# Hymba decoder step on one core: the order of the second norm and of the operand work inside a norm slot

## The chip, the cores and the metric

The kernel runs on one core of one Trainium2 chip. The metric is device time in microseconds (us) for one launch of the whole program, the span of the core's instructions and what lies around it. Below, PE is the matrix engine (TensorE), PEld its weight loads, DVE is VectorE, ACT is ScalarE, POOL is GpSimd, and SP is SyncE, which issues the DMAs.

## The reference

One decoder layer is computed for a prompt of 2048 tokens and for 8 x 4 sample tokens that share its weights (model width 1024). Attention and a spatial gate come first; their outputs are joined, multiplied by `w_out` and added to `x`. The part that the change touches follows:

```python
x = x + jnp.concatenate([att, u * gate], axis=-1) @ w_out
x = x + _swiglu(x, norm2_g, w_gate, w_up, w_down)

def _rmsnorm(x, g):
    y = x * lax.rsqrt(jnp.mean(x * x, axis=-1, keepdims=True) + EPS)
    return y * g

def _swiglu(x, g, w_gate, w_up, w_down):
    h = _rmsnorm(x, g)
    return (jax.nn.silu(h @ w_gate) * (h @ w_up)) @ w_down
```

A final norm of `x` gives the output. All of it is float32.

## The kernel before

Every float32 matrix is split into a high part and a rest (`xh` and `xl`, `wh` and `wl`), and a product is made of three matmuls: high by high, high by low, low by high. The gate and up products use a scheme with seven products of combined operands in the place of eight (`TOK` in `product` says which operand each takes). So each normed tile of 128 tokens must be turned (transposed), combined and split into seven high and seven low operands before the products can start.

The 16 tiles of 128 tokens are worked through in three blocks of 6, 6 and 4 tiles; the 32 sample rows are a fifth, small tile of the last block. For each block the program does this:

1. `open_unit` multiplies half 0 of `w_out` for each tile. The sums wait in PSUM banks (PSUM is the memory that PE writes its sums to).
2. `second_phase` goes over the tiles. In slot k it first calls `norm2_slot(B, k, order)`, then PE makes half 1 of the output product of tile `order[k]` (24 matmuls of 512 columns, `out_part`).
3. The units of the feed-forward part follow: `product` (lines 1669 to 1723) and `down_unit` (L1761 and L1763), which take most of the time of a block.

`norm2_slot` (L1538) works on two tiles at once. The tile `cur = order[k-1]` has its output product just done: `out_end` (L1441) adds it to `acc`, `norm2_square` (L1469 for the second half, L1474 for the whole tile) squares and sums on ACT, `rms_b` (L1450 and L1451 on DVE, then the root L1452 on ACT), `rms_c` (reciprocal and one Newton step, L142 to L146 on DVE) and `norm2_scale` (L1481 on ACT) give the normed tile in a buffer called `pair`. The other tile, `order[k-2]`, was scaled one slot earlier. `Operands` turns it on PE (8 transposes, L1493) into two PSUM banks `ps_t`, and makes its operands out of them:

- `first`: on ACT two copies (L1507, L1508), on DVE five subtractions (L1509 to L1513), which need the second of these copies and make the sums in two buffers called `zn`.
- `second` and `third`: on ACT the high parts of the sums (L135 twice) and of the second bank (L1518), on POOL the low parts (L138 twice).
- `last`: on DVE the low part of the second bank (L1526), which needs L1518.

What counts for the order: the program switches the automatic scheduling off with `manual_schedule`, and in the trace each engine starts its instructions in the order in which the code issued them, so that one which waits has all that stand behind it on its engine waiting too. Between two slots, other work is put into the same queues by `later` and `tick`: in block 0 the preparation of the first weights (`prepare`: on ACT L1618, on DVE L1602, L1605, L1608 and L1622, on POOL L1587, L1611 and L1622). In block 0 the first halves are added in this stretch too (`open_end`, another L1441, for tiles 2 to 5) and, for tiles 3 to 5, squared (`norm2_half`, L1462). After the last slot, `last_operands` does the operands of the last tile in steps of its own, through `first`, `second`, `third` and `last`.

Of the kernel before, what the change touches and what calls it, by code (L numbers as in the profile page):

```python
# [65 lines left out]
def hymba_step(ctx: ExitStack, tc: tile.TileContext, A: dict, O: dict):  # L66
# [73 lines left out]
    def newton(r, v):  # L140

        dve.reciprocal(r, r)  # L142
        if r.shape[-1] == 1:
            dve.tensor_scalar(v, v, r, r, op0=OP.mult, op1=OP.mult)  # L144
            dve.tensor_scalar(v, v, -0.5, 1.5, op0=OP.mult, op1=OP.add)
            dve.tensor_scalar(r, r, v, None, op0=OP.mult)  # L146
            return
        dve.tensor_mul(v, v, r)
        dve.tensor_mul(v, v, r)
        dve.tensor_scalar(v, v, -0.5, 1.5, op0=OP.mult, op1=OP.add)  # L150
        dve.tensor_mul(r, r, v)
# [14 lines left out]
    def zn_tile():  # L166
        return rp.tile([P, 512], F32, name="zn", tag="zn", bufs=3)
# [489 lines left out]
    def x_half_split(t, z):  # L657
# [6 lines left out]
    first = [("w", 0), ("x", 0, 0), ("w", 1), ("w", 2), ("w", 3), ("x", 1, 0), ("x", 2, 0), ("w", 4), ("x", 0, 1), ("w", 5), ("x", 1, 1),  # L664
             ("w", 6), ("x", 2, 1), ("w", 7), ("x", 3, 0), ("x", 3, 1)]
# [550 lines left out]
    for h in range(H):  # L1216
# [4 lines left out]
        if end:  # L1221

            x = s0 - NI
# [26 lines left out]
    for i, it in enumerate(items):  # L1250
        x, h, n = B0 + i, it["h"], it["n"]
# [66 lines left out]
    def square_tile():  # L1318
        return pair_tile(F32).rearrange("p a b -> p (a b)")
# [118 lines left out]
    def out_end(B, i, half, ps):  # L1438
        hs = slice(half * 512, (half + 1) * 512)
        if B.rows[i] == P:  # L1440
            dve.tensor_add(B.acc[i][:, hs], B.acc[i][:, hs], ps)  # L1441
        else:
            tmp = zn_tile()[0:SR]
            act.activation(tmp, ps[SR:2 * SR, :], AF.Copy)
            dve.tensor_add(B.acc[i][0:SR, hs], B.acc[i][0:SR, hs], ps[0:SR])
            dve.tensor_add(B.acc[i][0:SR, hs], B.acc[i][0:SR, hs], tmp)

    def rms_b(s1, n, more=None):
        if more is not None:
            dve.tensor_scalar(s1[:n, 0:1], s1[:n, 0:1], more[:n], None, op0=OP.add)  # L1450
        dve.tensor_scalar(s1[:n, 1:2], s1[:n, 0:1], 1.0 / D, EPS, op0=OP.mult, op1=OP.add)  # L1451
        act.activation(s1[:n, 2:3], s1[:n, 1:2], AF.Sqrt)  # L1452

    def rms_c(s1, n):
        v, r = s1[:n, 1:2], s1[:n, 2:3]
        newton(r, v)
        return r
# [19 lines left out]
    def norm2_scale(B, i, r):  # L1477
        n = B.rows[i]
        if n == P:
            B.xn[i] = square_tile()  # L1480
        act.activation(B.xn[i][:n], B.acc[i][:n], AF.Copy, scale=r)  # L1481

    class Operands:
# [16 lines left out]
                self.to = [x.rearrange("p (j k c) -> p j k c", j=7, k=4) for x in B.staged]  # L1500
            self.sums = [zn_tile()[:, 0:2 * 4 * (n // 2)].rearrange("p (j k t) -> p j k t", j=2, k=4) for _ in range(2)]

        def first(self):
            hi, lo_ = self.to
            (b11, b12), (b21, b22) = ((p_[:, 0], p_[:, 1]) for p_ in self.pts)
            (t1, t2), (t3, t4) = ((s_[:, 0], s_[:, 1]) for s_ in self.sums)
            act.activation(t4, b12, AF.Copy)  # L1507
            act.activation(hi[:, 0], b11, AF.Copy)  # L1508
            dve.tensor_sub(t1, t4, b11)  # L1509
            dve.tensor_sub(lo_[:, 0], b11, hi[:, 0].bitcast(F32))  # L1510
            dve.tensor_sub(t2, b22, t1)
            dve.tensor_sub(t3, b22, t4)
            dve.tensor_sub(t4, b21, t2)  # L1513

        def second(self):
            hi, lo_ = self.to
            split_sb(hi[:, 3:5], lo_[:, 3:5], self.sums[0])
            act.activation(hi[:, 1:3], self.pts[1], AF.Copy)  # L1518
# [9 lines left out]
    def place_staged(B):  # L1528

        for z, eng in enumerate((act, dve)):  # L1530
            src = B.staged[z].rearrange("p (m i c) -> p i m c", m=28, i=B.nt)
            dst = B.X[z].rearrange("p i (m w) -> p i m w", m=28)[:, :, :, 64:]
            if z:
                dve.tensor_copy(dst, src)
            else:
                act.activation(dst, src, AF.Copy)

    def norm2_slot(B, k, order):  # L1538

        n = len(order)  # L1540
        cur = order[k - 1] if 1 <= k <= n else None
        x = None
        if k == n and B.last:
            place_staged(B)
        if cur is not None:
            if cur in B.open:
                open_end(B, cur)
            out_end(B, cur, 1, B.half1.pop(cur))
        if 2 <= k:
            x = Operands(B, order[k - 2])  # L1550
            x.first()
        if cur is not None:
            s1, more = norm2_square(B, cur, zn_tile() if k == n and B.last else None)
        if x:
            x.second()
        if cur is not None:
            rms_b(s1, B.rows[cur], more)
            r = rms_c(s1, B.rows[cur])
        if x:
            x.third()  # L1560
        if cur is not None:
            norm2_scale(B, cur, r)
        if x:
            x.last()


# [244 lines left out]
    B = blocks[0]  # L1811
# [24 lines left out]
    def open_end(B, i):  # L1836
        out_end(B, i, 0, B.open.pop(i))
# [378 lines left out]
```

## Time and profile before

| what | value |
|---|---|
| median of 3 runs | 2546.14 us (2536.89 to 2548.04) |
| profiled execution: its time, its span | 2540.82 us, 2538.9 us |
| busy: PE | 2450.2 us, 97% of the span |
| busy: DVE, POOL, ACT | 1417.9 us (56%), 1379.3 us (54%), 1217.8 us (48%) |
| mean DMA rate | 189 GB/s |
| slots of the second norm: block 0, 1, 2 | about 955 to 992, 1541 to 1574, 2116 to 2142 us of the span |

The last row says where the transposes L1493 of the slots stand in the trace. A row of the timeline gives the start, the duration, the engine, the line, what is written and read, and in brackets the time that the engine sat idle before it, and what ended that. A busy PE is shown with modelled ends: two matmuls of a row overlap, and their starts are what counts.

### The profile page before, as it was taken

What the parts mean: (1) busy time and instruction counts of PE and PEld (TensorE: products, weight loads), DVE (VectorE), ACT (ScalarE), POOL (GpSimd) and SP (SyncE); (2) the same over time, 40 slices, a digit from 0 to 9 for tenths busy, and PEclk for the clock granted to TensorE, in tenths of its full rate; (3) what the DMA queues carried; (4) which work ended last, traced back from release to release, by engine and by line L of the source; (5) the groups of instructions that cost most, each with busy time, mean ns of one, the idle gap of its engine ahead of it and who ended that gap; (6) DMA issues with size and microseconds to landing.
All of it is one profiled execution on the core that took longest, in us unless ns stands there. A gap on an engine that the chain in (4) does not pass through costs nothing. (4 is left out here: it accounts for less than half of the span.)

```text
span 2538.9 us, 38949 instructions
## 1 busy us (share of the span) xinstructions
PE 2450.2 (97%) x13598; PEld 2171.0 (86%) x13598; DVE 1417.9 (56%) x2774; ACT 1217.8 (48%) x2579; POOL 1379.3 (54%) x1079
## 2 busy tenths in 40 slices
PE   8999989999999899999999999999999999999996
PEld 7787777678888878999999988999999988999995
DVE  4368685347888866444444475444444466444445
ACT  6424344346877747545545456323323336344432
POOL 1146643133677657767767644644645535676662
PEclk9999999999999999999999999999999999999998
DMA  8864944778688664644645563553644554665552
GB/s 269 248 193 130 296 122 141 229 256 245 196 239 239 170 201 154 211 158 163 203 137 191 166 203 116 207 199 129 214 155 166 198 162 132 224 215 193 195 199 98
DMA packets 313585, 480.00 MB, mean 189 GB/s; under 512 B 25889, under 2 KB 178882, under 8 KB 307502
## 3 DMA queue, kind: packets, MB, share of 16 engines
q1 hardware_dynamic: 308428, 469.00, 57.5%
q10 hardware_dynamic: 4962, 8.51, 1.1%
q8 instruction: 108, 1.77, 0.3%
q14 instruction: 87, 0.71, 0.1%
HBM read 381.72 MB, written 165.83 MB: 216 GB/s over the span
## 5 line engine op out<-in xcount | busy, mean ns | idle before, releaser
L1622 POOL TENSOR_TENSOR op<-fr,op 128x512 fp32r<-128x512 f32 x393 | 499.2, 1300 | 277.1 <-ACT op L1618 261.3
L1683 PE MATMUL ps_m<-xh,op 128*128 128x384 f32 (+5 forms) x1932 | 610.2, 316 | 0.2 <-POOL op L1622 0.2
L1681 PE MATMUL ps_m<-xh,op 128*128 128x384 f32 (+5 forms) x1932 | 610.1, 316 | 0.0
L1682 PE MATMUL ps_m<-xl,op 128*128 128x384 f32 (+5 forms) x1932 | 609.2, 315 | 0.0
L1761 PE MATMUL ps_o<-dw,hw 128*128 128x512 f32 x2040 | 481.4, 391 | 5.2 <-DVE acc L1763 5.2
L1761 PEld LDWEIGHTS ps_o<-dw,hw 128*128 128x128 f32 x2040 | 380.2, 188 | 84.7 <-DVE acc L1763 8.5
L1763 DVE TENSOR_TENSOR acc<-acc,ps_o 128x512 f32<-128x512 f32 (+1 forms) x362 | 247.8, 687 | 221.1 <-PE ps_o L1761 221.0
L1681 PEld LDWEIGHTS ps_m<-xh,op 128*128 128x128 f32 x1932 | 363.8, 188 | 4.0
L1682 PEld LDWEIGHTS ps_m<-xl,op 128*128 128x128 f32 x1932 | 363.6, 188 | 3.5
L1683 PEld LDWEIGHTS ps_m<-xh,op 128*128 128x128 f32 x1932 | 363.5, 188 | 0.8 <-POOL op L1622 0.8
L1728 ACT ACTIVATE ps_t<-zn 128x384 f32<-128x384 f32 (+2 forms) x132 | 60.0, 454 | 459.1 <-DVE zn L1711 346.1
L1618 ACT ACTIVATE op<-fr 128x512 fp32r<-128x512 f32 x396 | 235.2, 623 | 17.5 <-DMA fr<-ab_d 16.9
L138 POOL TENSOR_TENSOR dw<-fd,dw 128x1024 fp32r<-128x1024 f32 x65 | 156.3, 2405 | 121.0 <-ACT dw L135 120.9
L323 PE MATMUL ps_s<-wh,xh 128*128 128x512 f32 x480 | 196.8, 410 | 6.4 <-ACT xh L135 6.0
L324 PE MATMUL ps_s<-wl,xh 128*128 128x512 f32 x480 | 191.0, 398 | 0.0
L325 PE MATMUL ps_s<-wh,xl 128*128 128x512 f32 x480 | 190.6, 397 | 0.0
L1738 ACT ACTIVATE hw<-ps_t 128x384 fp32r<-128x384 f32 (+2 forms) x132 | 57.7, 445 | 176.6 <-DVE ps_t L1734 175.6
L1622 POOL TENSOR_TENSOR op<-pair,op 128x512 fp32r<-128x512 f32 x63 | 81.2, 1296 | 99.3 <-ACT op L1618 95.1
L323 PEld LDWEIGHTS ps_s<-wh,xh 128*128 128x128 f32 x480 | 92.3, 192 | 36.5 <-issue 8.6
L325 PEld LDWEIGHTS ps_s<-wh,xl 128*128 128x128 f32 x480 | 92.1, 192 | 20.5 <-DVE xl L138 0.3
L324 PEld LDWEIGHTS ps_s<-wl,xh 128*128 128x128 f32 x480 | 92.6, 193 | 17.9 <-DVE wl L226 0.5
L621 POOL TENSOR_TENSOR vl<-kv,vh 100x512 fp32r<-100x512 f32 (+1 forms) x32 | 44.5, 1393 | 110.0 <-ACT vh L615 84.3
(483 smaller groups left out, 4766.6 us busy)
## 6 DMA issues: line engine op xcount, KB each, us to landing
fr<-ab_d SPq DMA_DIRECT2D x308, 256.0 KB
fd<-in_w_down_dram SPq DMA_DIRECT2D x66, 512.0 KB
out_ks_dram<-in_cache_k_dram SPq DMA_DIRECT2D x56, 512.0 KB
out_vs_dram<-in_cache_v_dram SPq DMA_DIRECT2D x56, 512.0 KB
ab_d<-fr SPq DMA_DIRECT2D x88, 256.0 KB
raw<-in_w_in_dram SPq DMA_DIRECT2D x72, 256.0 KB
qk_d<-pair SPq DMA_DIRECT2D x64, 256.0 KB
ab_d<-pair SPq DMA_DIRECT2D x63, 256.0 KB
```

The costliest lines, as they stand in the source:

```text
L138: (eng_lo or pool).tensor_sub(lo, src, hi.bitcast(F32))
L323: pe.matmul(o[j], xh[:, k, :], wh, start=(k == 0), stop=False)
L324: pe.matmul(o[j], xh[:, k, :], wl, start=False, stop=False)
L325: pe.matmul(o[j], xl[:, k, :], wh, start=False, stop=(k == KD - 1))
L1618: act.activation(ops[f, j][0], ab[f][j], AF.Copy)
L1622: (pool if f or j else dve).tensor_sub(lo_, ab[f][j], hi.bitcast(F32))
L1681: pe.matmul(out, wh[:, ks], xh[:, :, k], start=(k == 0), stop=False)
L1682: pe.matmul(out, wh[:, ks], xl[:, :, k], start=False, stop=False)
L1683: pe.matmul(out, wl[:, ks], xh[:, :, k], start=False, stop=(k == 3))
L1728: act.activation(g, c, AF.Silu)
L1761: pe.matmul(ps[0:nr], l_, r_[:, cs], start=(z == 0 and y == 0), stop=(z == FC - 1 and y == len(pairs) - 1))
L1763: dve.tensor_add(B.acc[i][0:nr, cs], B.acc[i][0:nr, cs], ps[0:nr])
```

## The change

Inside a slot, the calls are put into another order. `first` is cut into three: `first_high` (the two ACT copies), `first_low` (three of the subtractions) and `first_sums` (the last two). The square of `cur` is now issued ahead of the other tile's copies, the first two instructions of `rms_b` ahead of its subtractions, the reciprocal, the Newton step and the scaling after three of these, and all of `second` and `third` behind the scaling. `first` itself, which `last_operands` uses, still issues the same seven instructions in the same order. No instruction is added or removed. Lines behind the edit are 13 or 14 higher in the new file (L1509 to L1513 become L1514, L1515, L1516, L1520 and L1521, L1518 becomes L1531, L1526 becomes L1539, L1618 becomes L1632).

```diff
--- before.py
+++ after.py
@@ -1500,17 +1500,30 @@
                 self.to = [x.rearrange("p (j k c) -> p j k c", j=7, k=4) for x in B.staged]
             self.sums = [zn_tile()[:, 0:2 * 4 * (n // 2)].rearrange("p (j k t) -> p j k t", j=2, k=4) for _ in range(2)]
 
-        def first(self):
+        def parts(self):
             hi, lo_ = self.to
-            (b11, b12), (b21, b22) = ((p_[:, 0], p_[:, 1]) for p_ in self.pts)
-            (t1, t2), (t3, t4) = ((s_[:, 0], s_[:, 1]) for s_ in self.sums)
+            return (hi, lo_, *((p_[:, z] for p_ in self.pts for z in range(2))), *((s_[:, z] for s_ in self.sums for z in range(2))))
+
+        def first_high(self):
+            hi, lo_, b11, b12, b21, b22, t1, t2, t3, t4 = self.parts()
             act.activation(t4, b12, AF.Copy)
             act.activation(hi[:, 0], b11, AF.Copy)
+
+        def first_low(self):
+            hi, lo_, b11, b12, b21, b22, t1, t2, t3, t4 = self.parts()
             dve.tensor_sub(t1, t4, b11)
             dve.tensor_sub(lo_[:, 0], b11, hi[:, 0].bitcast(F32))
             dve.tensor_sub(t2, b22, t1)
+
+        def first_sums(self):
+            hi, lo_, b11, b12, b21, b22, t1, t2, t3, t4 = self.parts()
             dve.tensor_sub(t3, b22, t4)
             dve.tensor_sub(t4, b21, t2)
+
+        def first(self):
+            self.first_high()
+            self.first_low()
+            self.first_sums()
 
         def second(self):
             hi, lo_ = self.to
@@ -1548,19 +1561,20 @@
             out_end(B, cur, 1, B.half1.pop(cur))
         if 2 <= k:
             x = Operands(B, order[k - 2])
-            x.first()
         if cur is not None:
             s1, more = norm2_square(B, cur, zn_tile() if k == n and B.last else None)
         if x:
-            x.second()
+            x.first_high()
         if cur is not None:
             rms_b(s1, B.rows[cur], more)
-            r = rms_c(s1, B.rows[cur])
         if x:
+            x.first_low()
+        if cur is not None:
+            norm2_scale(B, cur, rms_c(s1, B.rows[cur]))
+        if x:
+            x.first_sums()
+            x.second()
             x.third()
-        if cur is not None:
-            norm2_scale(B, cur, r)
-        if x:
             x.last()
```

DVE before, in block 0, from the last subtraction of slot 2 to the first addition of slot 3 (`zn`: sums of the tile whose operands are made; `s1`: sum of squares and root of the tile that is normed; `xl2`: low operands; `fr`, `op` and `raw`: weights in preparation; `acc2`: the next tile's sum):

```order
L1513 TENSOR_TENSOR zn_10249<-ps_t0_10243,zn_10248 128x256
L1450 TENSOR_SCALAR s1_10078<-s1_10078 128x1
L1451 TENSOR_SCALAR s1_10078<-s1_10078 128x1
L142 RECIPROCAL s1_10078<-s1_10078 128x1
L144 TENSOR_SCALAR s1_10078<-s1_10078 128x1
L145 TENSOR_SCALAR s1_10078<-s1_10078 128x1
L146 TENSOR_SCALAR s1_10078<-s1_10078 128x1
L1526 TENSOR_TENSOR xl2_9921<-ps_t0_10243,xh2_9920 128x512
L1605 TENSOR_TENSOR fr_10087<-fr_10087,fr_10089 128x512
L1622 TENSOR_TENSOR op_10219<-fr_10085,op_10219 128x512
L1608 TENSOR_TENSOR raw_10217<-fr_10087,fr_10085 128x512
L1441 TENSOR_TENSOR acc2_10233<-acc2_10233,ps_m1_9996 128x512
```

DVE after the change, between the same two places:

```order
L1516 TENSOR_TENSOR zn_10248<-ps_t0_10243,zn_10248 128x256
L142 RECIPROCAL s1_10078<-s1_10078 128x1
L144 TENSOR_SCALAR s1_10078<-s1_10078 128x1
L145 TENSOR_SCALAR s1_10078<-s1_10078 128x1
L146 TENSOR_SCALAR s1_10078<-s1_10078 128x1
L1520 TENSOR_TENSOR zn_10249<-ps_t0_10243,zn_10249 128x256
L1521 TENSOR_TENSOR zn_10249<-ps_t0_10243,zn_10248 128x256
L1539 TENSOR_TENSOR xl2_9921<-ps_t0_10243,xh2_9920 128x512
L1619 TENSOR_TENSOR fr_10087<-fr_10087,fr_10089 128x512
L1636 TENSOR_TENSOR op_10219<-fr_10085,op_10219 128x512
L1622 TENSOR_TENSOR raw_10217<-fr_10087,fr_10085 128x512
L1441 TENSOR_TENSOR acc2_10233<-acc2_10233,ps_m1_9996 128x512
```

The four instructions of the Newton step (L142 to L146) moved up past two subtractions. The low part (L1526, now L1539) stands where it stood, between them and the weight work, with the additions of the next slot behind it.

ACT before, in block 0, from the root of slot 4 to the square of slot 5 (`pair`: the scaled tile; `xh2`: high operands; `op_10428` is made out of a weight sum that POOL writes at L1611):

```order
L1452 ACTIVATE s1_10373<-s1_10373 128x1
L135 ACTIVATE xh2_9920<-zn_10400 128x512
L1481 ACTIVATE pair_10421<-acc3_10235,s1_10373 128x1024
L1618 ACTIVATE op_10428<-raw_10217 128x512
L1618 ACTIVATE op_10442<-fr_10089 128x512
L1462 ACTIVATE zn_10448,s1_10447<-acc4_10305 128x512
L1507 ACTIVATE zn_10474<-ps_t1_10463 128x256
L1508 ACTIVATE xh2_9920<-ps_t1_10463 128x256
L1469 ACTIVATE xh2_9920,s1_10447<-acc4_10305 128x512
```

ACT after the change, between the same two places:

```order
L1452 ACTIVATE s1_10373<-s1_10373 128x1
L1481 ACTIVATE pair_10414<-acc3_10235,s1_10373 128x1024
L135 ACTIVATE xh2_9920<-zn_10399 128x512
L1531 ACTIVATE xh2_9920<-ps_t0_10394 128x512
L135 ACTIVATE xh2_9920<-zn_10400 128x512
L1632 ACTIVATE op_10428<-raw_10217 128x512
L1632 ACTIVATE op_10442<-fr_10089 128x512
L1462 ACTIVATE zn_10448,s1_10447<-acc4_10305 128x512
L1469 ACTIVATE xh2_9920,s1_10447<-acc4_10305 128x512
```

The scaling (L1481) moved up past the two copies of sums (L135) and the copy of the second bank (L1518, now L1531), which all stand behind it now, ahead of the weights; the square (L1469) moved up past the next tile's two copies. On PE and SP no instruction changes its place. On POOL none does either, but its low parts (L138) stand ahead of weight work and wait for the copies that moved.

## The prediction

> **What bounds the kernel now.** I read the page first, for the engine that sets the end.
>
> ```profile
> span 2538.9 us, 38949 instructions
> PE 2450.2 (97%) x13598; PEld 2171.0 (86%) x13598; DVE 1417.9 (56%) x2774; ACT 1217.8 (48%) x2579; POOL 1379.3 (54%) x1079
> ```
>
> PE is busy for 97% of the span, so a change elsewhere counts only where PE waits for it, now or afterwards. The second view is what PE waits for between 955 and 1530 us; its first row is the one that the change touches. The third is the timeline of PE, cut to the transposes of block 0's slots (slots 2 to 6, then the last tile).
>
> ```profile
> PE ps_t L1493 <- ACT pair L1481: 3.8, 3, 1.6
> 955.00 1.03 PE L1493 MATMUL ps_t<-ident,pair 128*128 128x128 f32 x8
> 961.37 1.03 PE L1493 MATMUL ps_t<-ident,pair 128*128 128x128 f32 x8
> 968.58 1.09 PE L1493 MATMUL ps_t<-ident,pair 128*128 128x128 f32 x8 [0.69 <-ACT pair L1481]
> 976.69 1.09 PE L1493 MATMUL ps_t<-ident,pair 128*128 128x128 f32 x8 [1.54 <-ACT pair L1481]
> 984.87 1.09 PE L1493 MATMUL ps_t<-ident,pair 128*128 128x128 f32 x8 [1.60 <-ACT pair L1481]
> 991.55 1.04 PE L1493 MATMUL ps_t<-ident,pair 128*128 128x128 f32 x8
> ```
>
> A slot without a wait takes PE 961.37 - 955.00 = 6.37 us. The next three take 7.21, 8.11 and 8.18, and 3.8 us of that is PE waiting for the scaled tile. In block 1 PE has no such wait, in block 2 only one in front of slot 2, in a slot that has one tile and is not reordered. So the most that an earlier scaling can bring is 4.4 us, the excess of these three slots over 6.37: 0.17%. The question is what the work put behind the scaling does.
>
> **The cycle of one slot.** I take a slot of block 1, where nothing else is in the queues. First PE (the transposes of two slots), then DVE, then ACT; rows that no step uses are left out.
>
> ```profile
> 1560.50 1.04 PE L1493 MATMUL ps_t<-ident,pair 128*128 128x128 f32 x8
> 1566.85 1.04 PE L1493 MATMUL ps_t<-ident,pair 128*128 128x128 f32 x8
> 1560.70 0.69 DVE L1441 TENSOR_TENSOR acc<-acc,ps_o 128x512 f32<-128x512 f32 x1 [0.93 <-PE ps_o L1432]
> 1561.94 0.42 DVE L1509 TENSOR_TENSOR zn<-zn,ps_t 128x256 f32<-128x256 f32 x1 [0.56 <-ACT xh L1508]
> ...
> 1562.95 0.41 DVE L1512 TENSOR_TENSOR zn<-ps_t,zn 128x256 f32<-128x256 f32 x1
> ...
> 1564.64 0.16 DVE L142 RECIPROCAL s<-s 128x1 f32<-128x1 f32 x1 [0.51 <-ACT s L1452]
> ...
> 1565.47 0.68 DVE L1526 TENSOR_TENSOR xl<-ps_t,xh 128x512 fp32r<-128x512 f32 x1
> 1561.48 0.38 ACT L1508 ACTIVATE xh<-ps_t 128x256 fp32r<-128x256 f32 x1
> 1561.74 0.64 ACT L1469 ACTIVATE xh<-acc 128x512 fp32r<-128x512 f32 x1
> 1562.26 0.20 ACT L1469 ACTIVATION_READ_ACCUMULATOR xh<-acc 128x1 f32 x1
> ...
> 1563.91 0.60 ACT L1518 ACTIVATE xh<-ps_t 128x512 fp32r<-128x512 f32 x1 [0.22 <-DVE zn L1513]
> ...
> 1565.58 1.16 ACT L1481 ACTIVATE pair<-acc,s 128x1024 f32<-128x1024 f32 x1 [0.46 <-DVE s L146]
> ```
>
> Before, the addition L1441 waits 0.93 us for PE: DVE is ahead, and PE sets the pace (1566.85 - 1560.50 = 6.35). The scaling starts 1565.58 - 1560.70 = 4.88 us after the addition. Now I carry the same rows through the new order, with E for the start of the addition.
>
> - The square follows the addition: E + 0.72. The copies follow it: its step to the accumulator read is 0.52, the read holds ACT for about 0.1, so E + 1.34. The second copy starts 0.28 later and the subtractions 0.46 after that (1561.48 to 1561.94): E + 2.08. Mean square, root and copies run meanwhile: the accumulator is read by E + 1.44, and the two DVE instructions and the root end before the subtractions do.
> - Three subtractions take 1562.95 - 1561.94 = 1.01, so the reciprocal stands at E + 3.09. From it to the scaling is 0.94 (1564.64 to 1565.58): **E + 4.03**. The scaling is 0.85 us earlier. That is the gain.
> - Behind it on ACT: scaling 1.05 and copy 0.52 (the steps from 967.38 and in 968.96, rows below), then L1531, 0.60, ends at E + 6.20. DVE's low part L1539 waits for that, starts at E + 6.24, and DVE is free at **E + 6.84** (step of 0.60, as from 961.36 to 961.96, below). Before, it was free at 1565.47 + 0.60, E + 5.37.
>
> The next addition is queued behind L1539. So additions can follow each other no faster than every 6.84 us, and PE wants one every 6.35. **The change trades a scaling that is 0.85 us earlier for a cycle that is 0.49 us longer than PE's.** The head start is used up in the second slot; then PE waits, for the scaled tile and for L1539, which frees the PSUM bank that the next transposes write. What is late next is the addition, on DVE.
>
> **Block 1:** four steps from slot to slot, 4 x 0.49 = 1.96, of which the late bank takes PE's share in each: I carry **+1.9 us** at the last tile's transposes. **Block 2:** three such steps, 3 x 0.49 = **+1.5 us** (its first slot has the small tile and stays ahead of PE).
>
> **Block 0** has weight work in the same queues. DVE's, then ACT's, then POOL's rows:
>
> ```profile
> 955.46 0.68 DVE L1441 TENSOR_TENSOR acc<-acc,ps_o 128x512 f32<-128x512 f32 x1
> ...
> 960.44 0.99 DVE L1605 TENSOR_TENSOR fr<-fr 128x512 f32<-128x512 f32 x1
> 961.36 0.68 DVE L1622 TENSOR_TENSOR op<-fr,op 128x512 fp32r<-128x512 f32 x1
> 961.96 0.68 DVE L1608 TENSOR_TENSOR raw<-fr 128x512 f32<-128x512 f32 x1
> 962.56 0.67 DVE L1441 TENSOR_TENSOR acc<-acc,ps_m 128x512 f32<-128x512 f32 x1
> 963.16 0.68 DVE L1441 TENSOR_TENSOR acc<-acc,ps_o 128x512 f32<-128x512 f32 x1
> 963.87 1.06 ACT L1474 ACTIVATE xh<-acc 128x1024 fp32r<-128x1024 f32 x1 [1.20 <-DVE acc L1441]
> ...
> 967.38 1.15 ACT L1481 ACTIVATE pair<-acc,s 128x1024 f32<-128x1024 f32 x1 [0.46 <-DVE s L146]
> 968.43 0.61 ACT L1618 ACTIVATE op<-raw 128x512 fp32r<-128x512 f32 x1
> 968.96 1.14 ACT L1618 ACTIVATE op<-fr 128x512 fp32r<-128x512 f32 x2
> 970.00 0.62 ACT L1618 ACTIVATE op<-raw 128x512 fp32r<-128x512 f32 x1
> 970.52 0.62 ACT L1462 ACTIVATE zn<-acc 128x512 f32<-128x512 f32 x1
> ...
> 977.63 0.63 ACT L1618 ACTIVATE op<-raw 128x512 fp32r<-128x512 f32 x1 [1.00 <-POOL raw L1611]
> 973.68 2.69 POOL L138 TENSOR_TENSOR xl<-zn,xh 128x512 fp32r<-128x512 f32 x2 [2.01 <-ACT xh L135]
> 976.33 1.27 POOL L1611 TENSOR_TENSOR raw<-fr,raw 128x512 f32<-128x512 f32 x1
> ```
>
> - Slot 2: the addition is at 955.46, so DVE is free of L1539 at 962.3. Behind that stand the three weight operations (960.44 to 962.56: 2.12) and the first half's addition (0.60): the addition of slot 3 comes at 965.0, in place of 963.16. PE's own wait for slot 3 is 0.5 us, for the bank.
> - Slot 3 squares the whole tile (L1474, 0.43 longer), which now stands ahead of the copies: scaling at 969.4 to 970.6, before 967.38. L1539 ends at 972.3; the transposes, which have the bank 0.5 us after their start, count from 971.8 (before 968.58).
> - Slot 4: ACT is through with the copies at 972.0, four weight copies and the half's square take 2.09 + 0.62, and the square starts at 974.8. Scaling at 978.1, L1539 ends at 980.95: transposes at 980.4 (before 976.69).
> - Slot 5: POOL's two low parts now start behind the scaling, at 979.8, and end at 982.3. L1611 ends at 983.6; ACT waits for it as it did before, only longer, and squares at 985.3. Scaling at 988.6, L1539 ends at 991.5: transposes at 991.0 (before 984.87).
> - Slot 6: E at 992.0, scaling 996.0 to 997.2, L1539 ends at 998.9: the last tile's transposes count from 998.4 (before 991.55), 6.9 late.
>
> The same arithmetic with the old order gives the five starts of before within 0.2 us, late by that at the end; I take it off: **+6.7 us**. From there ACT and DVE are within 1 us and POOL within 3 us of where they stood relative to PE, which is less than the products leave them; and PE, busy to 97%, doesn't make up for what it lost.
>
> **Sum:** 6.7 + 1.9 + 1.5 = **+10.1 us**, 0.40%; the 3.8 us of waits removed are inside it, since the carried starts replace them. Against the profiled execution's own time, 2540.82, that is 2550.9. The runs shown lie around it (2536.89, 2546.14, 2548.04; with the profiled one their mean is 2543.0), so I predict 2543.0 + 10.1 = **2553 us**.
>
> **Bounds of what the trace doesn't show.** No row has an addition waiting behind L1526 for ACT. At the low end DVE and ACT would overlap as well as before and the excess of the three slots would go: -4.4 us. At the high end each of the 12 steps from slot to slot would be longer by 0.3 us (hand-overs between engines, 0.03 to 0.08 in the rows above, eight to a cycle): +4, so +14. I take the carried value, since the same rows, carried in the old order, reproduce 13 slots. Transposes, copies and subtractions keep their durations. DMAs and SP's order don't change; the stores that wait for L1605 and L1608 leave 2 us later, which I cost at nothing, as their loads are for weights that are used tens of us on.
>
> **Rivals.**
>
> 1. *The intended gain.* The waits go and nothing takes their place: 2543.0 - 4.4 = 2538.6. For it: ACT and DVE are about half busy in the span. Against it: L1539 stands between the scaling and the next addition in the order, and its release now comes 2 us later. 8%.
> 2. *Only block 0 pays.* Should a cycle be 0.5 us shorter than carried, blocks 1 and 2 hide it, and block 0 still has its weight work: 2543.0 + 5 to 7, say 2549. 15%.
> 3. *Half clock.* Two stretches of 3.4 us with their next ones, PE busy and granted clock:
>
> ```profile
> 868.70:872.10 3.40, 1.60 (x10) 1.00 0.38 80
> 872.10:875.50 3.40, 3.40 (x17) 0.50 0.93 218
> 981.50:984.90 3.40, 1.80 (x9) 1.00 0.50 142
> ```
>
>    After a stretch that is busy for 1.60 of 3.40, the clock is 0.50 for the next 3.4 us, which costs 1.7 us of matmul time; after the 1.80 of slot 5 it stayed 1.00. In my carry PE waits 3.6, 2.3 and 4.2 us in front of slots 4 to 6; the last leaves some stretch at 1.3 busy or less, wherever the stretches begin. Behind the first two waits PE has the next one to spare, 2.3 and 4.2 us, so a slower PE only waits less. Behind the third it has 0.8 us: +0.9, or with two such stretches +2.6. So 2554 to 2556. 22%. The Trainium skill, "TensorE: Matmul & The Clock Gate" (What's actually happening), says that after about 3.4 us of an idle window, in windows that run free of the program, the array goes to half clock until it was busy for one such window. By that rule only a wait that fills a window would count, and the rows show a drop with the array half busy; by the rule alone, +0.9 at the most.
> 4. *Slower, by POOL.* In slot 5 of block 0 the way to the square goes over three POOL operations in a row (L138 twice, L1611, 1.3 each). Were each 0.9 us longer, as POOL beside a busy DVE could be, +2.7, and the whole is past 12.7 us, where it counts as slower: 2556 and up. The tile's low parts are then late for PE's second product too, which has 1.9 us to spare. Against it: L138 takes 2.69 for two in the row above. 10%.
>
> The change does what it says: the order shows it.
>
> **How the numbers follow.** My forecast, +8 to +12, has 45%. 0.5% is 12.7 us, about what a measurement of this kernel can tell from no change. The runs of one kernel spread by 11 us, so of the forecast a fifth or more can be read as slower, of rival 3 two fifths, of rival 4 most: 0.31 slower. Faster by over 0.5% needs the intended gain and luck: 0.03. Within 0.5%: 0.66. The range goes from rival 2 in a low run (2542) to rival 3's upper end in a high run (2562) and leaves out rival 1 and what is past rival 4.
>
> **What will show it.** In the timeline after: scalings 4.0 us behind their additions in block 1; L1539 at E + 6.2; the addition following it with no wait for PE from the third slot on; transposes 6.8 apart; in block 0 waits for the scaled tile or the bank that sum to over 10 us, and transposes at 961.9, 971.8, 980.4, 991.0 and 998.4. Wrong if transposes in block 1 stay 6.4 apart, if the addition still waits for PE, or if PE's lateness behind block 0 shrinks in the products.

## The result, and the profile after

The changed kernel takes 2561.96 us (median of 6 runs, 2559.38 to 2570.99), the kernel before 2546.32 us beside it (6 runs, 2536.89 to 2548.04). The ratio is **1.007, with a 95% interval of 1.0056 to 1.0084**: slower by 17.8 us by the ratio, between 14 and 21 (the two medians lie 15.6 apart). The forecast was a loss of 10 us, within 0.5%; the loss is real, and larger than that. The profiled execution took 2563.01 us.

First the page of the changed kernel, its span and its busy times.

```profile
span 2561.2 us, 38963 instructions
PE 2462.3 (96%) x13598; PEld 2177.9 (85%) x13598; DVE 1423.2 (56%) x2774; ACT 1214.8 (47%) x2579; POOL 1378.9 (54%) x1079
```

The same matmuls as before keep PE busy 12.1 us longer (2462.3 and 2450.2), although none was added: more of them ran at a lower clock (mean granted clock 0.986, before 0.990). Half of that, 6.0 us, lies ahead of slot 2 of block 0, where nothing was moved; in block 0's slots it is 4.3 us. From slot 2 of block 0 to the last tile, before and then after (stretch, its length, PE busy, matmuls, granted clock, DMA share, GB/s):

```profile
955.00:992.00 37.00, 33.17 (x190) 1.00 0.52 164
```

```profile
963.90:1009.00 45.10, 37.50 (x190) 0.89 0.42 134
```

Then what PE waits for between 955 and 1530 us (us in total, times, longest):

```profile
PE ps_t L1493 <- ACT pair L1481: 5.4, 2, 2.9
...
PE ps_t L1493 <- DVE xl L1539: 2.2, 3, 1.2
```

The wait for the scaled tile, which the change was to shorten, has grown from 3.8 to 5.4 us, and a wait for L1539 has joined it. The timeline of PE, cut to the transposes of block 0's slots 2 to 6 and of the last tile:

```profile
963.89 1.03 PE L1493 MATMUL ps_t<-ident,pair 128*128 128x128 f32 x8
970.23 0.60 PE L1493 MATMUL ps_t<-ident,pair 128*128 128x128 f32 x4
971.14 0.63 PE L1493 MATMUL ps_t<-ident,pair 128*128 128x128 f32 x4 [0.31 <-DVE xl L1539]
980.14 1.11 PE L1493 MATMUL ps_t<-ident,pair 128*128 128x128 f32 x4 [2.87 <-ACT pair L1481]
981.96 1.09 PE L1493 MATMUL ps_t<-ident,pair 128*128 128x128 f32 x4 [0.71 <-DVE xl L1539]
990.13 1.03 PE L1493 MATMUL ps_t<-ident,pair 128*128 128x128 f32 x8
999.20 0.66 PE L1493 MATMUL ps_t<-ident,pair 128*128 128x128 f32 x4 [2.54 <-ACT pair L1481]
1001.02 1.08 PE L1493 MATMUL ps_t<-ident,pair 128*128 128x128 f32 x4 [1.17 <-DVE xl L1539]
1008.48 1.03 PE L1493 MATMUL ps_t<-ident,pair 128*128 128x128 f32 x8
```

Where eight transposes fall apart into four and four, the second bank came late, and I count from 0.5 us ahead of the second four, as the prediction did. (The same holds where the clock alone puts the second four more than 0.5 us behind the first; at half clock this adds 0.4 us to a tile's place.) From slot 2 to the last tile this is 44.6 us, against 36.55 before. Block 1, where the weight work is gone, shows the cycle itself (its first four slots):

```profile
1558.24 1.03 PE L1493 MATMUL ps_t<-ident,pair 128*128 128x128 f32 x8
1564.57 0.60 PE L1493 MATMUL ps_t<-ident,pair 128*128 128x128 f32 x4
1565.49 0.63 PE L1493 MATMUL ps_t<-ident,pair 128*128 128x128 f32 x4 [0.32 <-DVE xl L1539]
...
1572.38 0.63 PE L1493 MATMUL ps_t<-ident,pair 128*128 128x128 f32 x4 [0.32 <-DVE xl L1539]
...
1579.18 0.63 PE L1493 MATMUL ps_t<-ident,pair 128*128 128x128 f32 x4 [0.23 <-DVE xl L1539]
```

The second fours stand 6.89 and 6.80 us apart (1565.49, 1572.38, 1579.18), where PE's own work is 6.35. Why, is seen in one slot on DVE and on ACT (the slot of block 0 that starts at 963.89):

```profile
964.10 0.69 DVE L1441 TENSOR_TENSOR acc<-acc,ps_o 128x512 f32<-128x512 f32 x1
...
970.30 0.69 DVE L1539 TENSOR_TENSOR xl<-ps_t,xh 128x512 fp32r<-128x512 f32 x1 [1.43 <-ACT xh L1531]
970.91 0.79 DVE L1619 TENSOR_TENSOR fr<-fr 128x512 f32<-128x512 f32 x1
971.62 1.77 DVE L1636 TENSOR_TENSOR op<-fr,op 128x512 fp32r<-128x512 f32 x1
973.32 0.68 DVE L1622 TENSOR_TENSOR raw<-fr 128x512 f32<-128x512 f32 x1
...
974.52 0.67 DVE L1441 TENSOR_TENSOR acc<-acc,ps_o 128x512 f32<-128x512 f32 x1
```

```profile
968.12 1.15 ACT L1481 ACTIVATE pair<-acc,s 128x1024 f32<-128x1024 f32 x1 [1.84 <-DVE s L146]
969.18 0.61 ACT L135 ACTIVATE xh<-zn 128x512 fp32r<-128x512 f32 x1
969.69 0.58 ACT L1531 ACTIVATE xh<-ps_t 128x512 fp32r<-128x512 f32 x1
```

The scaling starts 4.02 us behind its addition (968.12 - 964.10), 0.86 earlier than the 4.88 of the slot of before that the prediction carried; in block 1 it is 4.00 to 4.10. But scaling, L135 and L1531 now hold ACT in a row, DVE sits idle for 1.43 us in front of L1539, and the next addition is queued behind it.

### The profile page after: what moved, and what is told of

It is laid out like the page before. It is cut to its first block, busy times and chain, and to the rows that moved or that the text cites. A ratio compares the mean times of both kernels' runs of the same rounds, so it can differ in the third digit from the quotient of the medians.

```text
span 2561.2 us, 38963 instructions
## 1 busy us (share of the span) xinstructions
PE 2462.3 (96%) x13598; PEld 2177.9 (85%) x13598; DVE 1423.2 (56%) x2774; ACT 1214.8 (47%) x2579; POOL 1378.9 (54%) x1079
## 3 DMA queue, kind: packets, MB, share of 16 engines
q8 instruction: 108, 1.77, 0.3%
## 5 line engine op out<-in xcount | busy, mean ns | idle before, releaser
L1636 POOL TENSOR_TENSOR op<-fr,op 128x512 fp32r<-128x512 f32 x393 | 499.1, 1300 | 276.0 <-ACT op L1632 265.9
L1695 PE MATMUL ps_m<-xh,op 128*128 128x384 f32 (+5 forms) x1932 | 610.6, 316 | 1.3 <-ACT xh L1549 1.3
L1695 PEld LDWEIGHTS ps_m<-xh,op 128*128 128x128 f32 x1932 | 364.3, 189 | 5.5 <-ACT xh L1549 1.5
L1632 ACT ACTIVATE op<-fr 128x512 fp32r<-128x512 f32 x396 | 235.3, 623 | 18.0 <-DMA fr<-ab_d 10.5
L138 POOL TENSOR_TENSOR dw<-fd,dw 128x1024 fp32r<-128x1024 f32 x65 | 156.3, 2405 | 122.2 <-ACT dw L135 120.3
L1636 POOL TENSOR_TENSOR op<-pair,op 128x512 fp32r<-128x512 f32 x63 | 81.2, 1295 | 100.5 <-ACT op L1632 96.3
```

The costliest lines, as they stand in the source:

```text
L138: (eng_lo or pool).tensor_sub(lo, src, hi.bitcast(F32))
L1632: act.activation(ops[f, j][0], ab[f][j], AF.Copy)
L1636: (pool if f or j else dve).tensor_sub(lo_, ab[f][j], hi.bitcast(F32))
L1695: pe.matmul(out, wh[:, ks], xh[:, :, k], start=(k == 0), stop=False)
```

## The experiments

**T**, the theory of the prediction: the copy L1531 stands behind the scaling on ACT, L1539 waits for it, and both the PSUM bank for the next transposes and DVE's next addition wait for L1539; so a cycle takes 6.8 us, and the losses follow. The rivals put the cause elsewhere: in POOL, whose low parts start later and meet DVE's work; in DVE's queue alone, whatever bank is freed; in the clock; or in the spread of the runs. Where tables give block 0, 1 or 2, the number is the time from slot 2's transposes to the last tile's; before, these are 36.55, 32.1 and 25.33 us.

### Both kernels once more, and each part alone

before_again and after_again are the two kernels unchanged. block0_only takes the new order where `B.b0 == 0` and the old one elsewhere; blocks12_only asks for `B.b0 > 0` in its place:

```diff
+        if B.b0 == 0:
...
+        else:
...
```

> The kernel before, run once more, to see how far one execution differs from another ahead of the first moved instruction. The theory (T): the changed order costs 13 us, all of it inside the slots of the second norm (block 0 +8.0, block 1 +1.9, block 2 +3.0 between the transposes of slot 2 and those of the last tile), and the 8.9 us by which the profiled execution of after was late at slot 2 of block 0 (963.9 against 955.0 us) is a difference between executions. By T this run is between 2537 and 2548 us, the three blocks take 36.6, 32.1 and 25.3 us within 0.3, and the transposes of slot 2 start anywhere from 952 to 965 us. The rival (S): the lateness ahead of slot 2 belongs to the changed program. By S they start within 2 us of 955.

> The changed kernel, run once more. T: blocks of 44.6, 34.0 and 28.3 us within 0.5 again, the transposes of slot 2 anywhere from 952 to 965 us, and a ratio to before of 1.005 to 1.006 (13 us). S: slot 2 at 962 us or later again, and a ratio of 1.007 to 1.009 (18 to 22 us).

> The new order of the slot in block 0 alone; blocks 1 and 2 keep the order of before. T: block 0 takes 44.6 us, blocks 1 and 2 take 32.1 and 25.3 as before; 8 us slower than before, ratio 1.003. The prediction's sizes would give 6.7 us, 43.4 in block 0. S: 8 us in the blocks and 3 to 9 more in front of them.

> The new order of the slot in blocks 1 and 2 alone. T: block 0 takes 36.6 us, blocks 1 and 2 take 34.0 and 28.3; 5 us slower than before, ratio 1.002. The prediction's sizes would give 1.9 and 1.5, 3.4 us in all. S: slot 2 of block 0 late by 3 to 9 us although block 0 is that of before.

| kernel | ratio, 95% interval | block 0 | block 1 | block 2 |
|---|---|---|---|---|
| before_again | 0.9998 (0.9986 to 1.001) | 36.55 | 32.08 | 26.93 |
| after_again | 1.007 (1.005 to 1.009) | 45.66 | 34.54 | 28.30 |
| block0_only | 1.0045 (1.0027 to 1.0062) | 45.95 | 32.11 | 25.33 |
| blocks12_only | 1.0032 (1.0021 to 1.0043) | 36.56 | 33.99 | 28.30 |

The difference comes back, it lies in the moved slots, and the parts add up within their intervals: 0.45% and 0.32% against 0.70%. Each block behaves as in the full change whichever order the others have. Block 0 alone costs 9.4 us by its trace, over the 6.7 of the prediction. T's sizes were too small here: it expected ratios of 1.005 to 1.006, 1.003 and 1.002 for the three changed kernels, and 44.6 us for block 0, which took 45.7 and 46.0. 1.007 is what S expected; slot 2, at 959.7 us, was not as late as S had it. (The 26.93 of before_again is one stretch at half clock in front of its second slot; the slots behind it are as before.)

### The order inside the slot

gap puts two copies of the operand part, the first L135 and L1531, back ahead of the scaling:

```diff
             x.first_low()
+            x.second()
         if cur is not None:
             norm2_scale(B, cur, rms_c(s1, B.rows[cur]))
         if x:
             x.first_sums()
-            x.second()
             x.third()
```

> The changed order, but the first copy of sums (L135) and the copy of the second bank (L1531) go back ahead of the scaling, where ACT waits 1.9 us for the Newton step anyway; the last two subtractions follow them. T (the scaling ahead of the bank copy makes L1539 late, and the next addition stands behind L1539): carried by the rows, the scaling starts 4.2 us after the addition, DVE is free 5.75 us after it, PE sets the pace again: slots 6.37 apart, block 1 at 32.1 us, block 2 at 25.3 to 25.9, and no waits for L1539. Block 0 keeps 2 us of its loss, 38.8, since its POOL copies still wait for the second sums. Ratio to before 1.000 to 1.002. R2 (the longer cycle comes from the square ahead of the copies, or from the Newton step between the subtractions, both still in): slots 6.8 apart, block 1 at 34.0, block 2 at 28.3, block 0 at 44 or more, ratio 1.005 to 1.007.

Ratio 1.0012 (1.0 to 1.0024). Blocks 0, 1 and 2 take 41.85, 31.96 and 26.2 us. In block 1 every wait is gone and the transposes stand 6.33 apart:

```profile
1547.89 1.03 PE L1493 MATMUL ps_t<-ident,pair 128*128 128x128 f32 x8
1554.22 1.03 PE L1493 MATMUL ps_t<-ident,pair 128*128 128x128 f32 x8
1560.55 1.03 PE L1493 MATMUL ps_t<-ident,pair 128*128 128x128 f32 x8
```

So it is these two copies behind the scaling, L1531 and the L135 in front of it, that lengthen the cycle: T. Block 2 was expected at 25.3 to 25.9 and is 0.9 us late, with a wait of 0.6 us for L1549 in front of its last tile, a line that comes back below. Block 0 was expected at 38.8 and is not repaired, though L1539 makes no wait there now. PE waits for the scaled tile instead (what it waits for between 955 and 1530 us):

```profile
PE ps_t L1493 <- ACT pair L1481: 6.2, 3, 2.8
```

That the chain over POOL (L138, L1611 of before) and the clock carry this rest I read from the timeline only; no run takes one of the two away.

low_deferred leaves the new order and moves L1539 itself behind the next slot's addition:

```diff
             out_end(B, cur, 1, B.half1.pop(cur))
+        if B.pending:
+            B.pending()
+            B.pending = None
...
-            x.last()
+            B.pending = x.last
```

> The changed order, but the low part L1539 is issued behind the next slot's additions, so that these wait for nothing on DVE. T: the addition is no longer late, but L1539 also frees the PSUM bank that the next transposes write; it now ends 1.3 us after the addition, and the second four transposes wait about 1.0 us for it in every slot: slots 7.3 apart, block 1 at 36 to 37 us, block 2 at 29 or more, ratio above that of the changed kernel by 0.002 to 0.004. Rival R3 (only the queue counts: the late addition alone is what the change costs): slots 6.4 apart, block 1 at 32.1, block 2 at 26.8, ratio 1.001 to 1.003.

Ratio 1.0083 (1.0065 to 1.0101): no better than the changed kernel, and by these intervals not told apart from it, where 0.002 to 0.004 more was expected. Block 1 takes 37.8 us, over the 36 to 37 expected, and block 2 30.3. The addition no longer waits for L1539, but PE does, in each slot, and the slots of block 1 stand 7.6 us apart, where 7.3 was expected (its transposes):

```profile
1564.35 0.63 PE L1493 MATMUL ps_t<-ident,pair 128*128 128x128 f32 x4 [1.03 <-DVE xl L1539]
...
1571.94 0.63 PE L1493 MATMUL ps_t<-ident,pair 128*128 128x128 f32 x4 [1.04 <-DVE xl L1539]
```

So the place of L1539 in DVE's queue is not the whole of it: the bank that it frees is a limit of its own, and whoever lets L1539 go later pays on PE.

square_first keeps the order of before, with the square alone moved ahead of the copies:

```diff
         if 2 <= k:
             x = Operands(B, order[k - 2])
-            x.first()
         if cur is not None:
             s1, more = norm2_square(...)
         if x:
+            x.first()
             x.second()
```

> One part of the change alone: the square of the tile that is normed goes ahead of the other tile's two copies on ACT; everything else stands as before. T, by the same carry: the subtractions start 0.84 us later, and as all five stand ahead of the root, the scaling comes 5.7 us after the addition in place of 4.9; PE waits for the scaled tile in each slot, not for L1526: slots 7.1 apart, block 1 at 35 to 36 us, block 2 at 28, block 0 at 40 to 42, ratio 1.004. R2 in its first form (the square alone makes up the change's cost): slots 6.8 apart, waits for the low part, blocks as in the changed kernel (44.6, 34.0, 28.3). If the square cost nothing: 36.6, 32.1 and 25.3.

Ratio 1.0035 (1.0022 to 1.0049); blocks 41.2, 34.35 and 27.3. Half of the loss thus comes with the first step of the change alone, and by another way: here no bank is late, and all waits of the transposes are for the scaled tile (955 to 1600 us):

```profile
PE ps_t L1493 <- ACT pair L1481: 8.3, 7, 2.7
```

With the square in front, copies, subtractions and high parts all come later and push the scaling back. Block 1 was expected between 35 and 36 and block 2 at 28; both did better, block 1 as one of its five steps took 6.55 us only.

### The long DVE instruction of block 0

L1636 took 1.77 us on DVE (971.62 above); the prediction carried 0.68. It ran beside POOL's low parts:

```profile
969.87 2.97 POOL L138 TENSOR_TENSOR xl<-zn,xh 128x512 fp32r<-128x512 f32 x2 [4.92 <-ACT xh L135]
```

They end at 972.84, and L1636 ends 0.55 us later. weight_on_pool moves this one instruction to POOL, as the other weight tiles have it:

```diff
-        (pool if f or j else dve).tensor_sub(lo_, ab[f][j], hi.bitcast(F32))
+        pool.tensor_sub(lo_, ab[f][j], hi.bitcast(F32))
```

> The changed kernel, with one weight operation (L1636 of the first weights, 1.77 us in the changed kernel's block 0 and 0.68 before) on POOL in the place of DVE. T: in block 0 it stands between L1539 and the addition of slot 3, so the addition and the transposes of slot 4 come 1.7 us earlier (slot 4 at 15.9 after slot 2 in place of 17.6), and block 0 ends 1 to 2 us earlier, at 42.6 to 43.6 or, with half clock behind a shorter wait, less. If DVE's queue were not the path there: 44.6 as in the changed kernel, or later since POOL has 1.3 us more. Blocks 1 and 2 as in the changed kernel, 34.0 and 28.3.

A miss: slot 4 stands at 17.0 us, where 15.9 was expected (17.6 in the changed kernel), block 0 at 44.3, the ratio at 1.0056 (1.0035 to 1.0076), not told apart from the changed kernel's. Block 2, expected at 28.3, takes 33.5 us; the last block's section below says why. DVE and POOL at that place:

```profile
969.01 2.99 POOL L138 TENSOR_TENSOR xl<-zn,xh 128x512 fp32r<-128x512 f32 x2 [5.00 <-ACT xh L135]
...
970.88 1.67 DVE L1622 TENSOR_TENSOR raw<-fr 128x512 f32<-128x512 f32 x1
971.96 1.74 POOL L1636 TENSOR_TENSOR op<-fr,op 128x512 fp32r<-128x512 f32 x1
972.47 0.68 DVE L1441 TENSOR_TENSOR acc<-acc,ps_m 128x512 f32<-128x512 f32 x1
```

The miss tells more than a hit would have: with L1636 gone, the next weight operation, L1622, is the long one. It took 0.68 in the changed kernel and takes 1.67 here, and again it ends 0.55 us behind POOL's L138 (972.00 and 972.55). It goes the other way too: POOL's second L138, issued while L1619 ran on DVE, took 1.74 us in the changed kernel, and the first 1.28. It isn't the instruction that is slow, but the place. The Trainium skill, "SBUF — State Buffer" (SBUF: two separate sides), says that a VectorE operation with two inputs in SBUF and a GpSimd operation that reads SBUF exclude each other: whichever starts first keeps the shared port pair to its end. Both rows agree with that, down to the same 0.55 us; L1441, which reads a PSUM bank, ran beside POOL's L1636 in 0.68. The profile before had the sign of it already, in a row that the prediction shows: L1605 took 0.99 us at 960.44, beside a POOL L138 that ended at 960.88, and it too ended 0.55 us later.

### The last block: a wait that nobody had carried

Block 2 lost 3.0 us in three steps in place of 1.5. First its last slot in the kernel before, PE and ACT (L1536 and L1681 are the L1549 and L1695 of the changed kernel):

```profile
2135.43 1.03 PE L1493 MATMUL ps_t<-ident,pair 128*128 128x128 f32 x8
2136.23 0.31 PE L1681 MATMUL ps_m<-xh,op 128*128 128x136 f32 x1
```

```profile
2135.45 0.58 ACT L1536 ACTIVATE xh<-xst 128x448 fp32r<-128x448 f32 x1 [0.26 <-PE ps_o L1431]
```

The same slot on PE, ACT, DVE and POOL of the changed kernel:

```profile
2155.49 1.36 PE L1493 MATMUL ps_t<-ident,pair 128*128 128x128 f32 x8
2158.11 0.33 PE L1695 MATMUL ps_m<-xh,op 128*128 128x136 f32 x1 [1.26 <-ACT xh L1549]
```

```profile
2157.48 0.58 ACT L1549 ACTIVATE xh<-xst 128x448 fp32r<-128x448 f32 x1 [1.61 <-POOL xl L138]
```

```profile
2157.48 0.40 DVE L1547 CAST xl<-xst 128x448 fp32r<-128x448 f32 x1 [1.41 <-POOL xl L138]
2157.79 0.68 DVE L1441 TENSOR_TENSOR acc<-acc,ps_o 128x512 f32<-128x512 f32 x1
```

```profile
2154.93 2.51 POOL L138 TENSOR_TENSOR xl<-zn,xh 128x512 fp32r<-128x512 f32 x2 [1.77 <-ACT xh L135]
```

`place_staged` (L1547 on DVE, L1549 on ACT) writes the small tile's operands into place and waits for POOL's last low part, which `third` now issues behind the scaling. DVE's addition is queued behind L1547 and comes late; and PE's first product of the next stage waits 1.26 us for L1549, a wait that the kernel before doesn't have. A wait of 0.62 us for L1539 in front of the last tile follows. staged_early issues `place_staged` in the fourth slot. What it leaves out: the squares of the tiles that follow then write over part of what was placed, so the small tile's products read other numbers; PE's matmuls are as many as before.

```diff
-        if k == n and B.last:
+        if k == 3 and B.last:
             place_staged(B)
```

> The changed kernel with the operands for the next stage (lines 1547 and 1549) placed in the last block's fourth slot instead of its last one. Theory (the third step of the last block is late because these two instructions stand behind GpSimd's late low parts): the last block's last tile stands at 26.5 to 27.0 us behind its slot 2 instead of 28.3, the wait of the first product behind it for L1549 is gone, blocks 0 and 1 are as in the changed kernel (44.6 to 46 and 34.0 to 34.6), ratio against the kernel before 1.006 to 1.0065. Rival (GpSimd's load as a whole delays the last tile, whatever the place of the two instructions): 28 us again and a wait of over 1 us for another line.

> Lines 1547 and 1549 in the fourth slot, for a further profile (the squares of the tiles that follow write over part of what they placed, so the small tile's products read other numbers). If the half clock belongs to the wait for L1549, which is gone here, the last tile of block 2 stands at 27.9 us and the clock is 1.00 behind it; if it comes in any kernel, half clock here as often as with the wait.

> As the run before it: 27.9 us with the clock at 1.00 if the half clock belongs to the wait for L1549.

Ratio 1.0043 (1.0029 to 1.0057), where 1.006 to 1.0065 was expected. The wait for L1549 is gone in all three profiles, but the last tile stands at 27.9, 27.6 and 27.8 us, not at 26.5 to 27: L1547 delays an addition at its new place too, and PE waits there (2110 to 2170 us of staged_early).

```profile
PE ps_t L1493 <- DVE xl L1539: 1.5, 2, 1.1
```

So the slots gain only 0.5 us on the changed kernel, yet the time gains 0.27% of it, some 7 us (1.0043 against 1.007, with intervals that barely overlap). What had gone with the wait, the next runs show.

### Where the last 4 us were

The moved slots of the first two profiles of the changed kernel are late by 13.0 and 14.6 us, and the ratio says 17.8. Slot 2 of block 0 also began late in them, at 963.9 and 959.7 us against 955.0 before, ahead of any moved instruction. Was that a draw, or did it belong to the change? before_c, after_c and after_d are the kernels once more, each for its profile.

> The kernel before once more, for its profile alone. If the time at which slot 2 of block 0 begins is one draw from the same spread in both kernels, it lies anywhere from 955 to 964 us here too; if the later begin belongs to the changed order, it lies at 955 to 957 as in the two profiles of this kernel so far.

> The changed kernel once more, for its profile alone. Draw from the same spread: slot 2 of block 0 begins anywhere from 955 to 964 us. Belonging to the changed order: at 959 or later, as in its two profiles so far (963.9 and 959.7). Both: last tile of block 0 44.5 to 46 us behind slot 2, block 1 34.0 to 34.6, block 2 28.3.

> As the run before it, a fourth profile of the changed kernel: slot 2 of block 0 at 955 to 964 us if the lateness is a draw, at 959 or later if it belongs to the changed order.

Slot 2 begins at 956.1, 955.3 and 956.4 us. The last two are the changed kernel's and settle it: a draw, and no part of the loss. Block 0 takes 46.3 and 45.9 us in them. But block 2 of after_c and after_d doesn't stand at 28.3; it takes 31.9 and 32.0 us. Stretches of PE behind the wait for L1549, for after_c and then for after_d (columns as above):

```profile
2149.00:2152.40 3.40, 2.00 (x17) 1.00 0.01 2
2152.40:2155.80 3.40, 3.40 (x19) 0.50 0.00 0
...
2159.20:2162.60 3.40, 3.40 (x18) 0.50 0.02 5
2162.60:2166.00 3.40, 3.40 (x33) 0.99 0.00 0
```

```profile
2149.20:2152.60 3.40, 2.01 (x17) 1.00 0.02 5
2152.60:2156.00 3.40, 3.40 (x18) 0.50 0.00 0
...
2173.00:2176.40 3.40, 3.40 (x18) 0.50 0.00 0
2176.40:2179.80 3.40, 3.40 (x32) 0.99 0.85 265
```

The wait of 1.3 us is the same as in the first two profiles. In these two, half clock follows it, for three stretches of 3.4 us and for seven. Seven stretches do 18 matmuls each where a full one does 32 or 33, so after_d loses 23.9 us times the missing 45%, some 10.6 us, to a wait of 1.3. The last runs asked whether it belongs to that wait: blocks12_b and blocks12_c have it, staged_b and staged_c (above) don't.

> New order in blocks 1 and 2 alone, for a further profile. If the half clock belongs to the wait of 1.3 us for L1549, it comes here in about half of the profiles: the last tile of block 2 at 28.3 us behind slot 2, or at 31 to 34 with a granted clock of 0.50 behind it; block 0 at 36.6 and block 1 at 34.0 in either case. If it comes in any kernel, no different from the run without the wait.

> As the run before it: 28.3 us, or 31 to 34 with half clock, each about as likely.

Block 2 takes 32.1 and 32.0 us in blocks12_b and blocks12_c, with half clock behind the wait in both (block 2 and what follows it are late by 13.6 and 7.1 us); in staged_b and staged_c the clock is 1.00. Over all profiles, half clock follows in **5 of 8 with the wait of 1.3 us, and in none of 10 without it** (gap, with a wait of 0.6, among the ten). It belongs to this wait in front of the product, and not to a wait's length alone: low_deferred, one of the ten, has one of 1.95 us inside block 2 and no half clock behind it. Whether it comes is drawn anew in each execution.

The traces show more of that draw. In all 18, every change of the clock lies on a grid of 3.413 us, within 0.004 us, and the grid stands elsewhere against the program in each execution. In the five profiles with the drop, the wait lies inside one stretch of the grid and ends 0.8 to 1.1 us ahead of the stretch's end. In the three without it, a grid line falls into the wait (after) or within 0.02 us of its end (after_again and blocks12_only). How busy PE was in the stretch doesn't tell the last two from the five: it is 2.0 of 3.4 us in all seven. This one, of after_again, holds the wait up to its end, and the clock stayed at 1.00 behind it:

```profile
2152.20:2155.60 3.40, 2.02 (x13) 1.00 0.18 65
```

No run here sets where the wait falls on the grid, so that this decides it is read from eight profiles and not tested.

With the half clock the account of the changed kernel closes. Each row is one profile, in us later than before:

| profile | block 0 | block 1 | block 2 | behind block 2's last tile | sum |
|---|---|---|---|---|---|
| after | 8.0 | 1.9 | 3.0 | 0.1 | 13.0 |
| after_again | 9.1 | 2.4 | 3.0 | 0.1 | 14.6 |
| after_c | 9.7 | 1.9 | 6.5 | 0.6 | 18.8 |
| after_d | 9.3 | 2.0 | 6.7 | 6.9 | 24.9 |
| mean | 9.0 | 2.1 | 4.8 | 1.9 | 17.8 |

The mean is the 17.8 us of the ratio; the agreement to the last digit is chance, as four profiles that reach from 13 to 25 don't fix a mean that well. What comes late between the blocks is left out: 0.6 to 0.9 us in the four, 0.4 and 0.7 in the two further profiles of the kernel before. No kernel tried here is faster than the one before: the most that the order could give back is 4.4 us, and the best new order, gap, is at 1.0012.

## Why the prediction was wrong

The sign held, and so did the mechanism of the cycle. What failed is the sum: block 2 was carried by the cycle alone, without a reader of the work that was moved back and without the clock behind that reader's wait, and block 0 was carried too small. Of the 7.7 us between the 10.1 carried and 17.8, block 2's slots have 3.3, the stretch behind them, which the sum put at nothing, 1.9, block 0 2.3 and block 1 0.2 (means of the four profiles). That the 2562 us measured are still the upper end of the range is in part luck: the kernel before measured 2546.3 beside them, 3 us over the 2543.0 that the forecast was counted from.

- **The cycle: right.** The scaling comes at E + 4.02 (E + 4.03 was carried), L1539 at E + 6.20 (E + 6.24), the addition follows without a wait for PE, and the cycle is 6.80 (6.84). In block 1, to which the prediction tied its signs, these are 4.00 to 4.10, 6.19 to 6.28 and 6.80 to 6.89. gap shows that the place of L1531, with the L135 in front of it, is the cause, low_deferred that the bank is a limit beside the queue.
- **Block 1: right.** +1.9 us was carried; the profiles have 1.9 to 2.4.
- **Block 0: mis-sized, 6.7 us carried and 8.0 to 9.7 measured.** "Transposes, copies and subtractions keep their durations" held, but the weight operations on DVE did not: between two additions 9.54 us were carried, and 10.42 came (964.10 to 974.52), since L1636 stood beside POOL's low parts. It reaches slot 4 as +0.8 (17.57 behind slot 2 in place of 16.8). From there to slot 6 the steps are 8.67 and 10.38, carried 8.6 and 10.6. The last step is 7.97 in place of 7.4, and 8.9 to 9.4 in the other three profiles: half clock behind the third wait (for 3.4 us in after, for 6.8 in the others), the prediction's third rival, which priced it at 0.9 to 2.6 us; the steps are 0.6 to 2.0 over the carried one. It was no rival: it came with the forecast, in each of the four profiles.
- **Block 2: the step that failed.** "Three such steps, 3 x 0.49 = +1.5 us" looked at the cycle alone. The first two steps were like that, and shorter: slots 4 and 5 are 0.3 and 0.6 us late, at 12.96 and 19.76. The third brought 2.4 more. The change moved `third`, and so POOL's low parts, past the scaling, and what waits for these, L1547 and L1549 in the last slot, was not named. The wait that comes of it costs 1.3 us, and where half clock follows, as in 5 of 8 profiles, 4 to 10.6 us more (after_c and after_d against the first two). The sum had both at nothing.
- **The third rival's place.** The prediction looked for half clock in block 0, where PE has spare time behind two of three waits. It priced none in block 2, where nothing behind the wait has time to spare. The Trainium skill, "TensorE: Matmul & The Clock Gate" (What's actually happening), has the drop follow at least one idle window of about 3.4 us and the return at least one busy window. The lengths agree with its window (three and seven times 3.4). The condition of the drop doesn't: a stretch busy for 2.00 of 3.40 was enough in after_c. Nor was one busy window enough for the return: seven wholly busy ones went by before it in after_d.
- **Ruled out:** the intended gain (no wait went without a longer one in its place), and the clock or the spread as the only cause (block 1 is late by 1.9 at a granted clock of 1.00 in the slots). POOL is a cause in part: the rival's longer chain did not come (L138 takes 2.5 to 3.0 us for two, 2.69 before), but POOL stretched an operation of DVE, and it released L1549 late.

What stays open: whether the wait's place on the clock's grid alone decides the drop, why half clock lasts three stretches in one execution and seven in another, and what carries block 0's rest in gap.

## What to carry to other kernels

When a chain is moved ahead on one engine, carry the cycle of every engine that the displaced work feeds: a result that is 0.86 us earlier was paid for with a cycle 0.45 us longer than that of the engine that sets the pace. Then go through every reader of what was moved back, the one-off ones at a block's end too: here it was a copy outside the loop whose wait of 1.3 us cost up to 12 with the clock behind it. And on an engine that is otherwise always busy, price a new wait with what the clock does behind it, not by its length.

## What was not expected of the hardware

- A wait of 1.3 us, in a stretch that was busy for 2.0 of 3.4 us, was followed by 10 or 24 us at a granted clock of 0.50 with PE wholly busy; in other executions of the same kernel by none.
- Every change of the granted clock, in all 18 profiles, lies on a grid of 3.413 us whose place against the program differs from one execution to the next. The same wait was followed by half clock where it lay inside one stretch of the grid, and by none where a grid line fell into it or on its end.
- A DVE operation on two SBUF tiles (128x512) took 1.77 or 1.67 us beside one of POOL's, and 0.68 elsewhere; both ended 0.55 us behind POOL's.
